# Moving one merge gate's projection from the fourth recurrence head's side work to the third's

## The chip, the cores and the metric

The kernel runs on one core of one Trainium2 chip. The metric is the device time of one execution in microseconds (us), the median of several runs; less is better. A profile of one execution gives what each engine did: PE (matrix multiply), DVE (vector), ACT (scalar and activation), POOL (GpSimd), SP (the engine that issues most transfers).

## What is computed

The kernel is one residual block over 1040 tokens (16 meta tokens and 1024 frames) of width 1024. The reference, cut to what matters here:

```python
u = _rmsnorm(h, norm_g[l])
proj = u @ w_in[l]                       # 6144 columns
(sb_q, sb_k, sb_v, sb_gate, hg_q, hg_f, hg_i, hg_gate, gate_sb, gate_hg) = jnp.split(proj, bounds, -1)
y_sb = _stick_breaking(sb_q, sb_k, sb_v) * jax.nn.silu(sb_gate)
o_hg = _group_rmsnorm(_hgrn2(hg_q, hg_f, hg_i, lb_all[l]), hg_norm_g[l])   # recurrence, 4 heads
y_hg = o_hg * jax.nn.silu(hg_gate)
merged = (jax.nn.sigmoid(gate_sb) * (y_sb @ w_sb_out[l])
          + jax.nn.sigmoid(gate_hg) * (y_hg @ w_hg_out[l]))                # 1024 + 1024 gate columns
h = h + merged @ w_out[l]
```

The recurrence of a head is S_t = diag(f_t) S_{t-1} + (1 - f_t) i_t^T, computed by doubling blocks (1, 4, 16, 32, 64, 128 tokens): each level multiplies keys and queries by products of forget gates on DVE, and forms a few small products on PE.

## The kernel before

Every float32 matrix product is done in three parts (high x high, high x low, low x high), so a weight block of 1024 x 128 columns is fetched raw (`wr`, by SP, L102), copied to its high part (`wh`, ACT L115) and its low part formed (`wl`, POOL L120). `wr`, `wh` and `wl` have two buffers each. A projection's matmuls are L259. A merge gate's projection is 48 matmuls of 512 columns into two PSUM tiles; ACT L994 applies the sigmoid, and L995 stores the result in DRAM. A head's forget-gate projection f is 72 matmuls of about 346 columns; ACT L780/L781 and POOL L783/L782 finish it.

Sixteen merge gates are wanted; ten are left for side work, five of them run beside the attention, and five (columns blocks 3 to 7 of `gate_hg`) beside the four recurrence heads. For each head `recurrence` gives a list of steps (main) and `stream` a list of quanta of three matmuls each (fill); `interleave` weaves the two by weights:

```python
target = base + span * m / total + lead
while fillq and done[0] < target:
    fw, ff = fillq.pop(0)
    ff()
    done[0] += fw
```

The fill of heads 0 to 2 is the next head's f projection and the gates in `some`; the fourth head's is its gates, then `split_all` (high and low parts of the attention's results, ACT L1028 and DVE L1029) and the first two products with `w_sb_out`. `stream` also loads the weights of the group that follows the one that begins. A scheduler then decides each engine's order from this text, and each engine keeps its order strictly.

In a head's main the names are: L858 (PE) the products of the levels 1 and 4 ("quads"), L874 those of level 16, L887 those of levels 32 and 64, L903 and L906 (DVE) the updates of keys and queries after each level, L942 to L950 the states, L962/L963 the outputs, L965 their copy, L834 a clear of the next head's matrix on POOL, L86/L87 a power on POOL, L972 the norm on DVE, L984 the transposes of the outputs in the next head.

After the heads come the products with `w_sb_out` and `w_hg_out`, and last the output product with `w_out` (L1270). The blocks of `w_out` are prepared in `direct(c)`, whose raw rows are fetched into the same two `wr` buffers (L1138), and whose first DVE operation is

```python
V.tensor_tensor(w12, w12, w11, op=ALU.subtract)     # L1150
put(3, BH[:, 3, c], BL[:, 3, c], w12)               # L1143 on ACT, L1144 on DVE
```

`direct` is written after the last head, but the scheduler places its DVE operations inside the third and the fourth head's lists. Its first transfer goes into the `wr` buffer of gate block 6, so it can't start before POOL has read that buffer for the last time (L120).

Of the kernel before, what the change touches and what calls it, by code (L numbers as in the profile page):

```python
# [45 lines left out]
def block_kernel(ctx: ExitStack, tc: tile.TileContext, x, meta, norm_g, w_in, w_sb_out,  # L46
# [218 lines left out]
    def stream(groups, nxt=None):  # L265
        q, pend = [], []
        for i, g in enumerate(groups):
            if "quanta" in g:
                q, pend = q + pend + g["quanta"], []
                continue  # L270
            follow = groups[i + 1] if i + 1 < len(groups) else nxt

            def first(g=g, follow=follow, state=[]):
                if not state:
                    state.append(1)
                    ensure(g)
                    if g["begin"]:
                        g["begin"]()
                    if follow is not None:
                        ensure(follow)  # L280
            qs = []
            for t0, n in g["pieces"]:
                qs += piece_quanta(g, t0, n, first)
            late, pend = pend, g["after"]
            for k, x in enumerate(late):
                qs.insert(4 + 3 * k, x)
            q += qs
        return q + pend
# [8 lines left out]
    def interleave(steps, lead=0.0):  # L297

        for _, fill in steps:
            fillq.extend(fill)  # L300
        for main, fill in steps:
            base = done[1]
            done[1] += sum(w for w, _ in fill)
            total = sum(w for w, _ in main)
            span = done[1] - base
            m = 0.0
            for w, fn in main:
                fn()
                m += w
# [5 lines that stand above are left out]
# [676 lines left out]
    def gate_group(gcol, e):  # L991
        def eg(acc, t0, n):
            sg = sb("sg", [P, 512])
            S.activation(sg, acc, AF.Sigmoid)  # L994
            nc.scalar.dma_start(gates[gcol, e][:, t0 - NM:t0 - NM + n], sg)  # L995

        return proj(gcol + P * e, REAL, eg)
# [88 lines left out]
    rest = [gate_group(C_GS, e) for e in range(N_GS, 8)] + [gate_group(C_GH, e) for e in range(8)]  # L1086
    share = FILL
    side, k0 = [], 0
    for p in range(4):
        own = ([pairs[1][1][1]], pairs[2][1], pairs[3][1], heads[0][1])[p]  # L1090
        some = rest[k0:k0 + share[p]]
        k0 += share[p]
        side.append(own[:1] + some[1:2] + own[1:] + some[:1] + some[2:])
    rest = rest[k0:]
# [12 lines left out]
    def hg_gate(h):  # L1107

        def emit():
            y = yhg[h]  # L1110
            g = sb("q", [P, SEQ])
            nc.sync.dma_start(g, kept_hg[h])
            V.tensor_tensor(y, y, g, op=ALU.mult)
        return (0.0, emit)

    tail = []
    for h in range(4):
        main, t = recurrence(h, heads[h][0], ("q", "ab", "v", "ab")[h])
        main = main[:1] + tail + main[1:]
        tail = t + [hg_gate(h)]  # L1120
        some, rest = (rest[:1], rest[1:]) if h < 3 else (rest, [])
        if h < 3:
            fill = stream(heads[h + 1][1] + some, heads[h + 2][1][0] if h < 2 else (rest + sbg)[0])
        else:
            fill = stream(some, sbg[0]) + [(0.0, split_all)] + stream(sbg[:2], sbg[2])
        interleave([(main, fill)], LEAD_B)
# [216 lines left out]
```

## Time and profile before

| | us |
|---|---|
| median of 3 runs | 902.82 (902.47 to 902.85) |
| the profiled execution | 903.0 |
| its span, first to last instruction | 901.3 |
| PE busy | 875.1 (97%) |
| DVE busy | 626.1 (69%) |

PE busy is an upper bound of real use, since matmuls overlap; but where PE is busy without a hole, what decides a stretch is the number of its matmuls. The profiled execution took 1.7 us more than its span.

### The profile page before, as it was taken

The numbers are of one execution on the slowest core, as the hardware profiler recorded it, in microseconds if no ns is written. First come the engines' busy times: TensorE is split into PE (matmuls) and PEld (weight loads), VectorE is DVE, ScalarE is ACT, GpSimd is POOL, SyncE is SP. The second block draws the span as 40 slices with busy tenths as digits, with TensorE's granted clock in tenths as the row PEclk, the third lists the DMA queues.
The fourth block names the chain that finished last, engine by engine and source line by source line (L and its number), as shares of the span: only waits on it lengthen the run. The fifth ranks groups of instructions, "written<-read, shape, count | busy, mean of one in ns | idle before, by whom it ended". The sixth has DMA issues, their size and how long they took to land. (4 is left out here: it accounts for less than half of the span.)

```text
span 901.3 us, 14988 instructions
## 1 busy us (share of the span) xinstructions
PE 875.1 (97%) x5672; PEld 753.5 (84%) x5672; DVE 626.1 (69%) x1081; ACT 408.0 (45%) x933; POOL 279.4 (31%) x303
## 2 busy tenths in 40 slices
PE   7999999999999999999999999999989999999996
PEld 5998888888889998898998898878877788888885
DVE  6893446555332468789788778867555788897886
ACT  7763333333332456546556556333435363223331
POOL 1026445544442212233211140526342000004552
PEclk9999999999999999999999999999999999999998
DMA  9223543333434312311321311232311466564212
GB/s 283 66 70 97 174 143 109 105 117 106 137 121 137 121 47 72 94 49 46 101 83 55 115 48 36 83 95 83 108 60 48 136 220 218 179 213 146 94 47 95
DMA packets 90587, 98.12 MB, mean 109 GB/s; under 512 B 6017, under 2 KB 65281, under 8 KB 90514
## 3 DMA queue, kind: packets, MB, share of 16 engines
q1 hardware_dynamic: 76688, 73.52, 26.9%
q10 hardware_dynamic: 13826, 23.64, 7.0%
q8 instruction: 45, 0.74, 0.4%
q14 instruction: 28, 0.23, 0.1%
HBM read 71.94 MB, written 25.20 MB: 108 GB/s over the span
## 5 line engine op out<-in xcount | busy, mean ns | idle before, releaser
L259 PE MATMUL acc<-uh,wh 128*128 128x346 f32 (+2 forms) x472 | 174.1, 369 | 0.0
L259 PE MATMUL acc<-ul,wh 128*128 128x346 f32 (+2 forms) x472 | 164.7, 349 | 0.0
L259 PE MATMUL acc<-uh,wl 128*128 128x346 f32 (+2 forms) x472 | 164.5, 349 | 0.0
L120 POOL TENSOR_TENSOR wl<-wr,wh 128x256 fp32r<-128x256 f32 x92 | 76.5, 852 | 281.0 <-ACT wh L115 253.4
L259 PEld LDWEIGHTS acc<-uh,wl 128*128 128x128 f32 x472 | 89.2, 189 | 7.0
L259 PEld LDWEIGHTS acc<-uh,wh 128*128 128x128 f32 x472 | 89.2, 189 | 5.3 <-issue 1.2
L259 PEld LDWEIGHTS acc<-ul,wh 128*128 128x128 f32 x472 | 89.6, 190 | 3.0 <-issue 0.4
L455 POOL TENSOR_TENSOR pw<-su,pw 128x512 fp32r<-128x512 f32 x44 | 59.2, 1367 | 43.3 <-ACT pw L454 43.3
L455 POOL TENSOR_TENSOR pw<-wr,pw 128x512 fp32r<-128x512 f32 x33 | 43.7, 1323 | 61.9 <-ACT pw L454 61.9
L628 ACT ACTIVATE ab<-z 128x456 f32<-128x456 f32 (+6 forms) x112 | 49.8, 448 | 26.5 <-PE z L626 26.0
L631 DVE TENSOR_TENSOR_SCAN ab<-ab,later 128x456 f32<-128x456 f32 (+3 forms) x64 | 55.6, 871 | 6.9 <-ACT ab L628 6.3
L466 PE MATMUL acc<-th,pw 128*128 128x512 f32 x176 | 58.0, 390 | 0.0
L671 DVE TENSOR_TENSOR wt<-tr,wt 128x384 fp32r<-128x384 f32 (+1 forms) x80 | 50.4, 630 | 10.1 <-ACT wt L670 7.9
L670 ACT ACTIVATE wt<-tr 128x384 fp32r<-128x384 f32 (+1 forms) x80 | 44.3, 555 | 26.0 <-PE tr L668 25.8
L682 PE MATMUL av<-wt,v 128*128 128x256 f32 x320 | 52.6, 286 | 3.6 <-DVE sg L689 3.1
L626 PE MATMUL z<-stk,q 128*128 128x456 f32 (+6 forms) x224 | 55.9, 331 | 0.0
L454 ACT ACTIVATE pw<-su 128x512 fp32r<-128x512 f32 x44 | 25.9, 626 | 60.9 <-DVE su L449 35.5
L682 PEld LDWEIGHTS av<-wt,v 128*128 128x128 f32 x320 | 46.2, 188 | 8.2 <-DVE sg L689 5.2
L635 DVE TENSOR_TENSOR_SCAN ab<-ab 128x348 f32<-128x348 f32 (+4 forms) x48 | 47.0, 980 | 7.2 <-ACT ab L628 5.8
L668 PE MATMUL tr<-ident,ab 128*128 128x128 f32 x288 | 45.3, 273 | 0.7 <-DVE ab L631 0.7
L115 ACT ACTIVATE wh<-wr 128x256 fp32r<-128x256 f32 x92 | 34.4, 412 | 22.0 <-PE acc L259 9.9
L626 PEld LDWEIGHTS z<-stk,q 128*128 128x128 f32 x224 | 38.3, 189 | 3.4
(360 smaller groups left out, 2031.1 us busy)
## 6 DMA issues: line engine op xcount, KB each, us to landing
wr<-in_w_in SPq DMA_DIRECT2D x48, 512.0 KB, 4.1
q<-q SPq DMA_DIRECT2D x32, 256.0 KB, 4.3
wr<-in_w_out SPq DMA_DIRECT2D x16, 512.0 KB, 3.6
sg<-gate SPq DMA_DIRECT2D x24, 256.0 KB, 3.4
gate<-sg ACTq DMA_DIRECT2D x20, 256.0 KB, 2.0
xb<-in_x SPq DMA_DIRECT2D x7, 512.0 KB, 8.3
gate<-co ACTq DMA_DIRECT2D x12, 256.0 KB, 2.0
pt<-hi SPq DMA_DIRECT2D x4, 520.0 KB, 3.3
```

Source lines behind the costliest of these rows:

```text
L120: eng.tensor_tensor(lo[:, cs], raw[:, cs], h[:, cs].bitcast(F32), op=ALU.subtract)
L259: T.matmul(acc, a, b, start=(k == 0), stop=(k == total - 1))
L455: G.tensor_tensor(t[:, 1], d[key], t[:, 0].bitcast(F32), op=ALU.subtract)
L466: T.matmul(acc, t[:, part // 2, c], (bh, bl, bh)[part][:, c], start=(c == part == 0), stop=(c == 3 and part == 2))
L626: T.matmul(z, qt[:, k, qo + qi * P:qo + (qi + 1) * P], st["k"][hh][:, c0:c1], start=(k == 0), stop=(k == 1))
L628: S.activation(a[:, c0:c1], z, AF.Sigmoid, scale=-1.0)
L631: ins = V.tensor_tensor_scan(w, w, later[:, WS - (n - c0):][:, ::-1], 1.0, op0=ALU.mult, op1=ALU.max)
L635: V.tensor_tensor_scan(w, w, w, a[:, c1:c1 + 1], op0=ALU.mult, op1=ALU.bypass)
L668: T.transpose(tp[:, c:c + P], self.w[qi][:, s0:s0 + P], ident)
L670: S.activation(wt[:, 0, lo:], tp[:, lo:], AF.Copy)
L671: V.tensor_tensor(wt[:, 1, lo:], tp[:, lo:], wt[:, 0, lo:].bitcast(F32), op=ALU.subtract)
L682: T.matmul(self.av, st["v"][hh][:, 2 * gg + j], wt[:, part, where[j]:where[j] + 256], start=(gg == g and part == 0 and j == 0), stop=False)
```

## The change

One more gate goes with the third head (h = 2), one fewer with the fourth (h = 3); the order of the gates stays.

```diff
         main, t = recurrence(h, heads[h][0], ("q", "ab", "v", "ab")[h])
         main = main[:1] + tail + main[1:]
         tail = t + [hg_gate(h)]
-        some, rest = (rest[:1], rest[1:]) if h < 3 else (rest, [])
+        n = (1,1,2,1)[h]
+        some, rest = rest[:n], rest[n:]
         if h < 3:
             fill = stream(heads[h + 1][1] + some, heads[h + 2][1][0] if h < 2 else (rest + sbg)[0])
```

No operation is added or removed. `interleave` now puts about 10 us more of fill weight (block 6) beside the third head, and the scheduler orders every engine anew from the third head's middle on. Lines after the diff have a number one higher than before: L1150 becomes L1151, L1144 becomes L1145.

On PE in the third head (products of level 16 and 32, `z`; `acc` with `wh_6779` is gate block 5, with `wh_6938` block 6). Before, the level 32 product came three matmuls into block 5's second half:

```order
L259 MATMUL acc_6948<-uh_72,wl_6780 128x512
L799 MATMUL tr_7072<-ident_63,pt_6773 16x128
L259 MATMUL acc_7075<-uh_72,wh_6779 128x512
L259 MATMUL acc_7075<-ul_73,wh_6779 128x512
L259 MATMUL acc_7075<-uh_72,wl_6780 128x512
L887 MATMUL z_7079<-wt_6313,stk_6310 32x32 x16
L259 MATMUL acc_7075<-uh_72,wh_6779 128x512
```

Now the level 16 product comes 21 matmuls into that half (the last four are shown):

```order
L259 MATMUL acc_7034<-uh_72,wl_6780 128x512
L259 MATMUL acc_7034<-uh_72,wh_6779 128x512
L259 MATMUL acc_7034<-ul_73,wh_6779 128x512
L259 MATMUL acc_7034<-uh_72,wl_6780 128x512
L874 MATMUL z_7056<-wt_6313,stk_6310 32x16 x32
L259 MATMUL acc_7034<-uh_72,wh_6779 128x512
L259 MATMUL acc_7034<-ul_73,wh_6779 128x512
L259 MATMUL acc_7034<-uh_72,wl_6780 128x512
L259 MATMUL acc_7115<-uh_72,wh_6938 128x512
```

Block 5's and block 6's other matmuls follow, so 18 matmuls stand between L874 and the level 32 product, and the small products come later against the fill.

On DVE in the third head (`stk` keys, `wt` queries, `wr_7820` the first raw rows of `w_out`). Before, the subtraction of `direct` stood ahead of the update of level 16:

```order
L903 TENSOR_TENSOR stk_6310<-stk_6310,ab_6761 128x65x8
L906 TENSOR_TENSOR wt_6313<-wt_6313,ab_6761 128x64x8
L866 COPY_PREDICATED dg_6758<-mask_651_4110,z_6952 128x16x12
L866 COPY_PREDICATED dg_6758<-mask_651_4110,z_6952 128x16x8
L866 COPY_PREDICATED dg_6758<-mask_651_4110,z_6952 128x16x4
L1150 TENSOR_TENSOR wr_7820<-wr_7820 128x512
L903 TENSOR_TENSOR stk_6310<-stk_6310,ab_6761 128x32x16
L906 TENSOR_TENSOR wt_6313<-wt_6313,ab_6761 128x32x16
```

Now it stands ahead of the updates of level 4:

```order
L908 TENSOR_TENSOR ab_6761<-ab_6761 128x8
L1151 TENSOR_TENSOR wr_7820<-wr_7820 128x512
L903 TENSOR_TENSOR stk_6310<-stk_6310,ab_6761 128x130x4
L906 TENSOR_TENSOR wt_6313<-wt_6313,ab_6761 128x128x4
L903 TENSOR_TENSOR stk_6310<-stk_6310,ab_6761 128x65x8
L906 TENSOR_TENSOR wt_6313<-wt_6313,ab_6761 128x64x8
```

It moved up by four updates and three masked copies. POOL's list is the same in both, row for row.

On DVE in the fourth head (`wr_7833` the next raw rows of `w_out`, L926 and L947 of the states), the second subtraction now stands like this; before, it stood ahead of L926, and L947 had other work before it:

```order
L1145 TENSOR_TENSOR ul_7819<-wr_7822,uh_7818 128x512
L903 TENSOR_TENSOR stk_6772<-stk_6772,ab_7291 128x8x64
L906 TENSOR_TENSOR wt_6775<-wt_6775,ab_7291 128x8x64
L1145 TENSOR_TENSOR ul_7819<-wr_7820,uh_7818 128x512
L926 COPY v_7635<-tr_7636 16x128
L1054 TENSOR_TENSOR pt_7488<-acc_7512,sg_7302 128x256
L1151 TENSOR_TENSOR wr_7833<-wr_7833 128x512
L947 COPY stk_7652<-av_7653 128x128
```

Its buffer is the one that the first row shown here reads last.

## Rows read from the trace of the kernel before

**Rows 1.** The page, busy time: engine, us, share of the span, instructions.

```profile
PE 875.1 (97%) x5672; PEld 753.5 (84%) x5672; DVE 626.1 (69%) x1081; ACT 408.0 (45%) x933; POOL 279.4 (31%) x303
```

**Rows 2.** Windows, third and fourth head: length, engines' busy us, granted clock, DMA share, GB/s.

```profile
645.60:692.00 46.40, 42.11 (x453) 35.08 (x452) 27.55 (x53) 19.12 (x49) 17.82 (x17) 0.96 0.20 66
692.00:748.60 56.60, 55.59 (x499) 44.87 (x499) 46.26 (x94) 25.19 (x66) 5.03 (x5) 1.00 0.51 168
```

**Rows 3.** Waits of PE, 640 to 760 us: total us, times, longest.

```profile
PE z L887 <- DVE wt L906: 3.7, 1, 3.7
PE tr L984 <- DVE ab L972: 1.6, 2, 1.0
```

**Rows 4.** Chain of waits (whole, and of 660 to 680 us): start, us, what.

```profile
665.04 2.09 POOL wl L120 x3
...
667.15 4.27 DMA wr<-in_w_out
...
673.46 0.70 PE z L887 x32
...
748.61 66.84 PE acc L259 x288
```

**Rows 5.** Windows around two waits of PE; columns as in rows 2.

```profile
669.75:673.46 3.71, 0.00 (x1) 0.01 (x1) 1.95 (x4) 0.00 (x0) 0.00 (x0) 1.00 0.06 25
674.08:677.53 3.45, 3.45 (x15) 2.67 (x9) 1.29 (x2) 2.02 (x6) 0.00 (x0) 0.53 0.20 78
696.20:699.20 3.00, 1.99 (x73) 1.61 (x72) 3.00 (x4) 1.10 (x2) 0.00 (x0) 1.00 0.23 87
```

**Rows 6.** Timeline of PE in the third head.

```profile
652.14 0.66 PE L984 MATMUL tr<-ident,ab 128*128 128x128 f32 x4 [0.58 <-DVE ab L972]
...
660.44 0.40 PE L259 MATMUL acc<-uh,wh 128*128 128x512 f32 x1
...
668.80 0.48 PE L259 MATMUL acc<-uh,wh 128*128 128x512 f32 x1
...
674.08 0.66 PE L259 MATMUL acc<-uh,wh 128*128 128x512 f32 x1
...
677.93 1.15 PE L887 MATMUL z<-wt,stk 128*64 128x64 f32 x16
```

**Rows 7.** Timeline of POOL in the third head.

```profile
653.64 0.62 POOL L782 TENSOR_SCALAR stk<-stk,omlb,lb 128x348 f32<-128x348 f32 x1
...
661.03 0.74 POOL L120 TENSOR_TENSOR wl<-wr,wh 128x256 fp32r<-128x256 f32 x1 [1.31 <-ACT wh L115]
...
662.88 2.16 POOL L782 TENSOR_SCALAR stk<-stk,omlb,lb 128x346 f32<-128x346 f32 x1
```

**Rows 8.** Timeline of DVE in the third head.

```profile
654.15 1.23 DVE L1113 TENSOR_TENSOR ab<-ab,q 128x1024 f32<-128x1024 f32 x1 [0.51 <-ACT ab L985]
...
659.42 1.00 DVE L908 TENSOR_TENSOR ab<-ab 128x65 f32<-128x65 f32 x4
...
664.01 0.68 DVE L906 TENSOR_TENSOR wt<-wt,ab 128x512 f32<-128x512 f32 x1
...
671.51 0.69 DVE L1150 TENSOR_TENSOR wr<-wr 128x512 f32<-128x512 f32 x1 [5.92 <-DMA wr<-in_w_out]
```

**Rows 9.** Timelines of the fourth head: PE, DVE, SP's queue, ACT.

```profile
697.41 1.09 PE L984 MATMUL tr<-ident,ab 128*128 128x128 f32 x8 [1.01 <-DVE ab L972]
...
708.52 0.89 PE L858 MATMUL z<-wt,stk 128*32 128x48 f32 x64
...
704.57 0.45 DVE L848 TENSOR_TENSOR wt<-wt,ab 128x256 f32<-128x256 f32 x1
...
707.12 0.76 DVE L120 TENSOR_TENSOR wh<-wl,wh 128x256 fp32r<-128x256 f32 x2
...
721.28 2.14 SPq L1138 DMA_DIRECT2D wr<-in_w_out  x2
...
725.48 0.63 ACT L1143 ACTIVATE uh<-wr 128x512 fp32r<-128x512 f32 x1 [0.65 <-DMA wr<-in_w_out]
```

## The prediction, made before the changed kernel ran

> **What bounds the kernel now.** I began with the page: PE is busy 97% of the span [rows 1], so most of the time is set by the number of its matmuls, which the change leaves alone. What it can move is holes in PE, and the rate at which matmuls go. So I read the stretch of the heads next, by windows. The third head's window has 46.40 us with PE busy 42.11, and it alone shows a granted clock below 1.00 [rows 2]. The fourth has PE busy 55.59 of 56.60, with DVE busy 46.26, so there DVE has 10.3 us to spare. The waits of PE in this stretch name three holes, all ended by DVE: one of 3.7 us ahead of L887 and two ahead of L984, 1.6 us together, the larger 1.0 [rows 3]. After the last head PE runs 288 matmuls back to back in 66.84 us [rows 4], 0.232 us each; this step of a 512-column matmul is used below.
>
> The chain of waits tells where the 3.7 us come from [rows 4]: POOL ends three L120 (low parts of gate block 6's weights) at 667.13; only then is their raw buffer free, and SP's transfer of `w_out` rows takes 4.27 us into it; DVE, whose next instruction in order is L1150, stands still for it for 5.92 us and starts it at 671.51 [rows 8]; behind it come the two updates, and the level 32 product starts at 673.46 [rows 4]. PE had run out of matmuls placed ahead of that product.
>
> The hole costs more than itself. In the window of the hole PE does nothing for 3.71 us; in the next, 674.08 to 677.53, the granted clock is 0.53, so mostly the lower level, 1.2 GHz, in place of 2.4 [rows 5]. Nine matmuls fill 674.08 to 677.93 [rows 6]: 3.85 us, where nine steps of 0.232 and some 0.2 for the changes between block kinds make 2.3. That is 1.5 us lost. Around the fourth head's hole of 1.0 us the clock stays at 1.00 [rows 5].
>
> **The change, part by part.** It adds no instruction and removes none, no transfer either: 48 matmuls (11.1 us of PE) stand in the third head rather than the fourth. PE's total is the same, so the sum is made of holes and of the slow clock.
>
> *The third head's first hole* (0.58 us ahead of L984 [rows 6]). L984 now comes after 15 matmuls of the second piece of f rather than 8; the seven more, of 346 columns, are over 1 us of work. DVE is ready at the old time, since nothing ahead of it moved. Gain 0.6 us.
>
> *The third head's large hole.* DVE's subtraction moved up by four updates, so DVE waits longer; what counts is when it is released and what PE still has then. f's last matmul is followed by the first of block 5 at 660.44 [rows 6]; without the first hole that is 659.9. From there to the first L120 of block 6 POOL needs 0.6 us, and to the start of L782 another 1.85 [rows 7]: 662.3. L782 took 2.16 us here and 0.62 for 348 columns at 653.64. The longer one ended at 665.04, as L906 of DVE (from 664.01, 0.68) ended its run of four updates [rows 8]; at 653.64 to 654.15 DVE was idle but for 0.1 us [rows 8]. In the new order DVE stands waiting from about 661 (its small products ended at 660.42 [rows 8], and L1113 ahead of them moves back by some 0.5), so no update runs beside L782: I take 0.62. Then three L120, 2.1 us, to 665.0, and the transfer, 4.27, to 669.3. From the release of L1150 to the small product took 671.51 to 673.46, 1.95 us, with two updates between [rows 4, 8]; now four stand between, at 0.61 each two more: 3.2 us. L874 can start at 672.6. PE gets there when? Block 5's first half with its small blocks took 660.44 to 668.80, 8.36 us [rows 6], of which one small block of the kind of L887's 0.70 [rows 4] now stands later: 7.6. Then 21 matmuls, 4.9: 659.9 + 12.5 = 672.4. So a hole of 0.2 us in place of 3.7, with no slow clock, since even 1.0 us brought none. If L782 takes 2.16 all the same, the hole is 1.7. Gain 3.7 + 1.5 - 0.2 = 5.0 us; low end 3.5 less a slow clock if it comes, 2.0; high end 5.2.
>
> The Trainium skill, page SBUF — State Buffer, section SBUF: two separate sides, says that POOL and a DVE operation with two SBUF inputs take one pair of ports by an exclusive lock, the loser blocked for the whole instruction. The two rows of L782 agree with it; without such a rule the sum would keep 2.16 and stand 1.5 us higher.
>
> *The fourth head's hole ahead of L984* (1.01 [rows 9]). It lies between L832 and L984, with the chain POOL clear, POOL power, L972 between, and 15 matmuls to cover it, in both orders. No change.
>
> *The fourth head's thinner cover.* Here the 48 matmuls are missing, and DVE's chain meets PE at more places. Ahead of the second product of quads there were 39 matmuls after L984, 11.1 us to L858 [rows 9]; 12 fewer make 8.3. DVE ended L848 at 705.02, 7.6 us after L984 began; now two L120 (0.68 in steps [rows 9]) stand ahead too: 8.3. A hole of 0 to 0.2, I take 0.1. Between L874 and the second L887 PE has 21 matmuls, 4.9 us, and the first L887; DVE has some 14 operations, five of them updates or low parts more than the chain needs, about 6.0 against 5.7: 0.3. Last, the second subtraction: SP's transfer was issued at 721.28 and first used at 725.48, 4.2 us later [rows 9]; DVE now reaches it 2.4 us after the buffer is free, so it waits about 1.8 us ahead of L947 and the states. PE has its transposes and some 10 matmuls there, about as much as DVE needs: 0.3, and up to 1.8 if these come out shorter. Together 0.7 us, from 0 to 2.5.
>
> *After the heads* the same matmuls follow in the same order. DVE is a few low parts behind there, some 2 to 3 us; three PSUM tiles of 2.8 us each stand between it and PE. I cost it at nothing; if that cover is gone, it costs up to 1 us.
>
> The sum: 903.0 - 0.6 - 5.0 + 0.7 = 898.1. The profiled execution stood 0.2 us above the median, so the median should be **898.0** (rounded up), 0.53% below 902.8. A difference of 0.2% (1.8 us) is about what a measurement of this kernel can tell from no change.
>
> **Rivals.**
> 1. *POOL stays slow*, or the transfer lands 1.5 us later than 4.27: a hole of 1.7 us ahead of L874. 899.5 without the slow clock, 901.0 with it. For it: L782 ran 2.16 once; against it: DVE has nothing to run beside it in the new order. Chance 0.14.
> 2. *The fourth head's waits add up*: three close places with errors the same way, and the second subtraction at its upper price: 899.7, or 901.2 if one of them lets the clock fall. For it: DVE at 46.26 of 56.60 [rows 2], in a window that loses 11.1 us. Chance 0.13.
> 3. *Slower: DVE becomes the bound of the fourth head.* If all of its 10.3 us of idle time stayed (waits for PE's small products, POOL's power, the transfer), the head would not get shorter at all by the matmuls that left: 903 - 5.6 + 11.1 = 908.5. The point from which it decides: the head would take 46.3 us and what stays of the idle, against 45.5 in the sum; over 6.6 us of the 10.3 must stay to end above 904.6. Against it: six or so of the low parts of `w_out` and two of the attention's results leave that stretch of DVE's list. Chance 0.04.
> 4. *No change*: the wait only goes to another place, DVE standing at L1151 until some 676 rather than 669.3, a hole ahead of L874 of 3.7 us with its slow clock, 903 less the 0.6: 902 to 903. It needs a release 3.5 us later than my steps give, such as another transfer ahead of this one in SP's queue; before, the queue waited for nothing but the buffer. Chance 0.05.
>
> **Numbers.** The forecast, the hole gone and 0 to 1.5 us given back in the fourth head (897.0 to 899.3), has 0.64. Range 896.8 to 901.0: it takes in the first two rivals but for their worst ends, and leaves out about 0.15. Faster by over 0.2% (below 901.0): 0.64, nearly all of the first rival and most of the second: 0.84. Within 0.2%: 0.12. Slower: 0.04.
>
> **What would show it.** In the profile after: the third head's window at clock 1.00 with no hole over 0.5 us; DVE idle ahead of L1151 for some 8 us, longer than before; L782 beside it at 0.6 to 0.9; the transfer issued near 665 and landed near 669; L874 near 672.5; the fourth head with PE's hole of 1.0 ahead of L984, and small ones ahead of L858, L887 and L963. Wrong would be: a clock below 1.00 in either head, a hole of over 1.5 us ahead of L874, or DVE's second wait for `w_out` followed by a hole of PE.

## The result and the profile after

The changed kernel takes **897.4 us** (median of 4 runs, 896.82 to 899.36) against 902.84 of the kernel before (4 runs beside it, 902.47 to 904.4): ratio 0.9939, 95% interval 0.9925 to 0.9953. The forecast was 898.0, its range 896.8 to 901.0. The profiled execution took 896.8, with a span of 895.1, 6.2 us less than the 901.3 of before.

The page's busy times (us, share of the span, instructions) answer to [rows 1], the waits of PE from 640 to 760 us (in all, times, longest) to [rows 3]:

```profile
PE 873.3 (98%) x5672; PEld 752.4 (84%) x5672; DVE 625.9 (70%) x1081; ACT 406.9 (45%) x933; POOL 279.2 (31%) x303
```

```profile
PE tr L984 <- DVE ab L972: 1.1, 1, 1.1
```

The wait of 3.7 us ahead of L887 is gone, and of the two ahead of L984 the fourth head's alone is left. The windows of the two heads, cut at the same instructions as [rows 2] (length, then PE, PEld, DVE, ACT, POOL, clock, DMA share, GB/s):

```profile
645.30:694.80 49.50, 49.50 (x493) 41.50 (x492) 28.32 (x53) 20.17 (x51) 17.50 (x17) 1.00 0.23 78
694.80:742.30 47.50, 46.31 (x459) 37.30 (x459) 41.26 (x88) 22.34 (x64) 5.47 (x5) 1.00 0.48 156
```

Before, the heads took 46.40 + 56.60 = 103.0 us; now 49.5 + 47.5 = 97.0. Nearly the whole difference arises here: the third head begins 0.3 us earlier (645.30 against 645.60), which the change does not explain, and behind the fourth head 152.7 us were left before (901.3 - 748.6), and 152.8 are now (895.1 - 742.3). Of the 48 matmuls, 40 cross the cut between the two windows (x453 to x493, x499 to x459), which is 9.3 us of PE. The third head has PE busy in all of its 49.50 us, at clock 1.00 where it had been 0.96.

The steps of the prediction can be followed in the timelines of PE, POOL, SP's queue and DVE, in this order:

```profile
652.23 0.60 PE L984 MATMUL tr<-ident,ab 128*128 128x128 f32 x4
...
671.81 0.74 PE L874 MATMUL z<-wt,stk 128*32 128x16 f32 x64
...
700.25 0.66 PE L984 MATMUL tr<-ident,ab 128*128 128x128 f32 x4 [1.09 <-DVE ab L972]
...
656.76 2.19 POOL L782 TENSOR_SCALAR stk<-stk,omlb,lb 128x346 f32<-128x346 f32 x1
...
661.83 0.63 POOL L782 TENSOR_SCALAR stk<-stk,omlb,lb 128x346 f32<-128x346 f32 x1
662.43 2.11 POOL L120 TENSOR_TENSOR wl<-wr,wh 128x256 fp32r<-128x256 f32 x3
...
664.57 0.33 SPq L1139 DMA_DIRECT2D wr<-in_w_out  x1
...
657.93 0.68 DVE L906 TENSOR_TENSOR wt<-wt,ab 128x512 f32<-128x512 f32 x1
...
668.06 0.69 DVE L1151 TENSOR_TENSOR wr<-wr 128x512 f32<-128x512 f32 x1 [7.33 <-issue]
...
670.49 0.68 DVE L906 TENSOR_TENSOR wt<-wt,ab 128x512 f32<-128x512 f32 x1
...
724.53 0.42 DVE L1054 TENSOR_TENSOR pt<-acc,sg 128x256 f32<-128x256 f32 x1 [1.03 <-PE av L940]
724.87 0.68 DVE L1151 TENSOR_TENSOR wr<-wr 128x512 f32<-128x512 f32 x1
```

DVE's wait for `w_out` did not go away: it is longer than before, 7.33 us against 5.92 [rows 8], and PE does not wait behind it. The trace puts it down to "issue"; I take the transfer issued at 664.57 and first read at 668.06 for what ended it, since the subtraction reads nothing but its rows.

### The profile page after: what moved, and what is told of

Same layout as the page of the kernel before. It is cut to its first block, busy times and chain, and to the rows that moved or that the text cites. A ratio compares the mean times of both kernels' runs of the same rounds, so it can differ in the third digit from the quotient of the medians.

```text
span 895.1 us, 14985 instructions
## 1 busy us (share of the span) xinstructions
PE 873.3 (98%) x5672; PEld 752.4 (84%) x5672; DVE 625.9 (70%) x1081; ACT 406.9 (45%) x933; POOL 279.2 (31%) x303
## 4 chain that ended last, share of the span: by engine, by line
PE 86%; DVE 8%; ACT 3%; issue 1%; POOL 1%; DMA 1%; ACTq 0%; DVEq 0%; POOLq 0%
PE acc L259 34%; PE acc L466 10%; PE z L466 7%; PE tr L466 7%; PE acc L1271 4%; PE av L682 3%; PE tr L668 3%; PE z L626 3%; PE tr L1271 3%; PE z L1271 2%; PE acc L350 2%; DVE ab L635 2%; DVE ab L631 1%; PE z L963 1%; PE z L962 1%
## 5 line engine op out<-in xcount | busy, mean ns | idle before, releaser
L259 PE MATMUL acc<-uh,wh 128*128 128x346 f32 (+2 forms) x472 | 173.4, 367 | 0.0
L259 PE MATMUL acc<-ul,wh 128*128 128x346 f32 (+2 forms) x472 | 164.1, 348 | 0.0
L259 PE MATMUL acc<-uh,wl 128*128 128x346 f32 (+2 forms) x472 | 163.6, 347 | 0.0
L120 POOL TENSOR_TENSOR wl<-wr,wh 128x256 fp32r<-128x256 f32 x92 | 76.0, 846 | 273.4 <-ACT wh L115 245.7
L259 PEld LDWEIGHTS acc<-uh,wl 128*128 128x128 f32 x472 | 88.8, 188 | 6.8
L259 PEld LDWEIGHTS acc<-uh,wh 128*128 128x128 f32 x472 | 88.9, 188 | 4.7 <-issue 0.8
L259 PEld LDWEIGHTS acc<-ul,wh 128*128 128x128 f32 x472 | 89.2, 189 | 3.3 <-issue 0.8
```

Source lines behind the costliest of these rows:

```text
L120: eng.tensor_tensor(lo[:, cs], raw[:, cs], h[:, cs].bitcast(F32), op=ALU.subtract)
L259: T.matmul(acc, a, b, start=(k == 0), stop=(k == total - 1))
```

## Experiments

The theory: the gain is the hole of 3.7 us that DVE's wait for `w_out` left in PE, with the slow clock behind it and the small hole ahead of the third head's L984; the longer third head covers the wait. The rivals: more matmuls in the third head are worth something for themselves; the wait only changes its place. All ratios stand against runs of the kernel before on the same chip (902.84 us for the changed kernel, 903.32 for the first four runs, 903.47 for the last three), so runs of different rows are compared by their ratios.

| | us (runs) | ratio, 95% interval |
|---|---|---|
| changed kernel | 897.40 (4) | 0.9939, 0.9925 to 0.9953 |
| one: before, subtraction held | 898.28 (5) | 0.9945, 0.9933 to 0.9958 |
| two: changed, subtraction held | 897.63 (5) | 0.9942, 0.9929 to 0.9954 |
| three: gates 1, 1, 3, 0 | 910.47 (5) | 1.0078, 1.0064 to 1.0091 |
| four: gates 1, 0, 2, 2 | 901.09 (11) | 0.9976, 0.9967 to 0.9984 |
| five: gates 1, 2, 1, 1 | 900.75 (5) | 0.9968, 0.9956 to 0.9981 |
| six: three updates more | 899.96 (6) | 0.9965, 0.9953 to 0.9977 |
| seven: six updates more | 903.64 (11) | 0.9996, 0.9986 to 1.0006 |

**One: take the wait away and leave the gates.** In the kernel before, the first `direct` is held back until the fourth head's first DVE operation has been issued (lines from there on carry numbers one or two higher):

```diff
+            if hd == 3:
+                late.append(ins)
...
-        direct(e - 4)
+        if e == 4:
+            with tc.issue_after(late[0].ins):
+                direct(0)
+        else:
+            direct(e - 4)
```

> The gates stay as before (one, one, one, two); only the first subtraction of w_out and what follows it are held back until the fourth head's first DVE operation, so the third head's DVE list holds no wait for a transfer. Theory (the gain is the hole of 3.7 us at that wait and the slow clock behind it, 1.5): the hole ahead of L887 and the clock of 0.53 are gone, the 0.6 us ahead of the third head's L984 stays, so 902.8 - 5.2 = 897.6, up to 899 where the fourth head pays for the subtraction. Rival (the gain comes from 48 more matmuls in the third head, whatever DVE waits for there): 902 to 903.

898.28 us, and the ratio cannot be told from the changed kernel's. The waits of PE (640 to 760 us), the windows of the third and the fourth head, and the timelines of PE and DVE:

```profile
PE tr L986 <- DVE ab L974: 1.6, 2, 1.0
```

```profile
645.70:687.00 41.30, 40.71 (x458) 34.06 (x457) 27.19 (x52) 19.11 (x49) 17.85 (x17) 1.00 0.22 74
687.00:743.80 56.80, 55.67 (x499) 44.74 (x499) 46.74 (x95) 25.20 (x66) 5.07 (x5) 1.00 0.52 168
```

```profile
652.32 0.66 PE L986 MATMUL tr<-ident,ab 128*128 128x128 f32 x4 [0.59 <-DVE ab L974]
...
701.62 0.68 DVE L1152 TENSOR_TENSOR wr<-wr 128x512 f32<-128x512 f32 x1
```

The hole ahead of the level 32 product is gone without moving a gate, the 0.59 ahead of the third head's transposes stays, and the subtraction, now in the fourth head, waits for nothing. The third head takes 41.30 us against 46.40, at a clock of 1.00, and the fourth is as long as before. The transfer itself is issued at 667.34, as before (667.15), so what moved is DVE's place for it. So the gain is the wait's, not that of the third head's added matmuls.

**Two: the same hold in the changed kernel** (gates 1, 1, 2, 1).

> The changed kernel with the same hold: DVE no longer stands 7.3 us at the subtraction in the third head. Theory (the longer third head covers that wait, it costs nothing): the time of the changed kernel, 897.4, within 0.2%. Rival (the covered wait still takes something, later in DVE's list or in the clock): 895.5 or less. On the side: if the 0.63 us of L782 comes from DVE standing idle beside it, it takes about 2.1 us here, beside DVE's updates, and if it comes from something else, 0.63 again.

897.63 us: the covered wait costs nothing that these runs can tell. The question on the side came out against the reason that I gave. DVE and POOL in the third head:

```profile
665.35 0.70 DVE L905 TENSOR_TENSOR stk<-stk,ab 128x520 f32<-128x520 f32 x1 [4.25 <-PE z L860]
...
662.21 0.63 POOL L782 TENSOR_SCALAR stk<-stk,omlb,lb 128x346 f32<-128x346 f32 x1
```

L782 takes 0.63 us here too, but DVE does not update beside it: without the subtraction it waits 4.25 us for the second product of quads (L860 with the hold, L858 in the kernels without it), which the added matmuls have moved behind L782.

**Three: all three gates in the third head, none in the fourth** (`n = (1,1,3,0)[h]`).

> All three remaining gates' matmuls in the third head, none in the fourth. The fourth head's stretch of 45.3 us loses another 11.1 us of PE, to 34.2, with DVE busy for 39.1 there in the changed kernel, of which some 3 are low parts that leave with the gate. Theory (a head costs the longer of PE and DVE's busy time plus a few small waits): the stretch takes 37 to 40, the kernel 900.5 to 903.5. Rival 3 of the prediction (DVE's idle time there stays whole): the stretch stays at 45.3, the kernel at 908. If the matmuls leave without a price: 897.4.

910.47 us: my theory missed by 7 us, and rival 3's 908 is near. The heads' windows, with the same columns as above, then the waits of PE (700 to 760 us), and the chain behind the largest on ACT, POOL and PE:

```profile
645.70:706.80 61.10, 61.10 (x542) 50.60 (x541) 31.48 (x59) 23.72 (x59) 17.98 (x17) 1.00 0.27 87
706.80:754.20 47.40, 39.79 (x420) 30.89 (x420) 38.22 (x84) 17.89 (x53) 5.30 (x5) 0.96 0.38 116
```

```profile
PE tr L984 <- DVE ab L972: 4.6, 2, 3.2
PE acc L259 <- DVE wt L1029: 1.5, 1, 1.5
```

```profile
710.85 0.31 ACT L969 ACTIVATE sg<-ab 128x128 f32<-128x128 f32 x1 [2.74 <-DMA gate<-sg]
...
712.65 0.20 POOL L86 TENSOR_SCALAR s<-s 128x8 f32<-128x8 f32 x1 [4.12 <-ACT sg L969]
...
715.92 0.77 PE L984 MATMUL tr<-ident,ab 128*128 128x128 f32 x5 [3.24 <-DVE ab L972]
```

The third head grew by the gate, 49.5 to 61.1; the fourth did not get shorter, 47.4 against 47.5. But DVE is not full there (38.22 of 47.40); PE stands idle for 7.6 us (1.2 in the changed kernel), and the clock falls to 0.96. The largest hole ends a chain: the last gate's store out of `sg` is issued only at 706.15, just before the head begins; ACT waits 2.74 us for it before it may write its sums of squares into `sg`, POOL's power comes behind these, then L972, then PE. In the changed kernel the chain has no such wait, beside about as many matmuls (15 there, 14 here), and costs 1.09 us against 3.24. The matmuls that stand here in place of a gate's are products with `w_sb_out`, which wait for DVE themselves (the 1.5 ahead of L259), and five more waits, of 0.31 to 1.34 us, join. That a gate's matmuls would have covered all of these is argued; no run takes them one by one.

**Four: none in the second head, two in the third and fourth** (`n = (1,0,2,2)[h]`).

> The third head keeps two gates as in the changed kernel, the fourth has two as before, the second none. The first subtraction of w_out stands later in DVE's list. Theory: no hole at a wait for w_out; the second head (38.6 us, PE 37.9, DVE 24.9) goes to 27.5 of PE, less than the busy time of DVE and the small waits of its chain allow: 897.4 plus 1 to 4 us of holes there, 898.4 to 901.4. Rival (the spread of the gates alone decides, two in the third are enough): 897.4.

901.09 us, within the theory's 898.4 to 901.4: two gates in the third head are not enough by themselves. PE waits 1.13, 0.25 and 0.92 us in the second head and 1.72 ahead of the third's L984; no wait of PE for `w_out` is among them. The theory had put all of the holes into the second head; what lengthened the 1.72 was not tried.

**Five: the fourth head's gate to the second** (`n = (1,2,1,1)[h]`).

> The fourth head's gate goes to the second head, the third keeps one as before. The first subtraction of w_out then stands at the third head's start in DVE's list, ahead of the first products of gates. Theory (the gain is the wait that leaves the place ahead of L887, wherever the gate goes): no hole ahead of L887 and a clock of 1.00; the second head's hole ahead of L984 (0.7) goes as well, the third's of 0.6 stays: 897 to 898.5. Rival (a wait for w_out only changes its place): a hole ahead of the third head's L984 of 2 us or more, 900 to 903.

900.75 us, which is the rival's outcome, though not by its cause. POOL at the third head's start, and DVE and PE behind it:

```profile
657.26 0.95 POOL L834 MEMSET ab<- 128x1024 f32 x1
658.18 1.92 POOL L120 TENSOR_TENSOR wl<-wr,wh 128x256 fp32r<-128x256 f32 x2
660.18 0.20 POOL L86 TENSOR_SCALAR s<-s 128x8 f32<-128x8 f32 x1
...
662.19 1.23 DVE L972 TENSOR_TENSOR ab<-ab,s 128x1024 f32<-128x1024 f32 x1 [3.38 <-POOL s L87]
663.55 0.74 DVE L1151 TENSOR_TENSOR wr<-wr 128x512 f32<-128x512 f32 x1
...
663.47 1.12 PE L984 MATMUL tr<-ident,ab 128*128 128x128 f32 x4 [2.31 <-DVE ab L972]
```

The subtraction waits for nothing. But the added gate's low parts, two L120 of 1.92 us together, now stand in POOL's list between the clear and the power, so L972 is late and PE has a hole of 2.31 us, with a slow clock behind it. ACT's last sum was there at 658.64 and the power started at 660.18, so these low parts account for some 1.5 us of the hole. Where a gate goes decides what its side work collides with; the wait for `w_out` was removed here as well.

**Six and seven: a hole of chosen length.** In the changed kernel, three or six more updates ahead of the third head's L874 (each x = max(x, x) on the queries, which changes no value):

```diff
+            if hd == 2 and h == 4:
+                for _ in range(3):
+                    V.tensor_tensor(qv, qv, qv, op=ALU.max)
```

> The changed kernel with three more updates of 0.61 us each (x = max(x, x) on the queries, values unchanged) on DVE ahead of the third head's L874. With the three masked copies that now stand ahead too (0.67), DVE releases L874 2.5 us later; some 0.6 us were to spare, so a hole of 1.9 us. Theory (the clock falls behind long holes only: 1.72 us left it at 1.00 in the run with no gate in the second head, 3.24 and 3.71 did not): clock 1.00, 897.5 + 1.9 = 899.4. Rival (any hole longer than those of 1.0 to 1.1 us costs the clock too): 900.9.

> The same with six: L874 4.5 us later, a hole of 3.9 us. Theory (a hole as long as the one of before takes the clock with it, another 1.5 us): the granted clock near 0.53 for about 3.5 us behind the hole, 897.5 + 3.9 + 1.5 = 902.9. Rival (a hole costs only itself, and the 1.5 us had another cause): 901.4.

PE's L874 in the timeline, and the window behind the hole, with three more updates:

```profile
674.20 0.74 PE L874 MATMUL z<-wt,stk 128*32 128x16 f32 x64 [1.75 <-DVE wt L906]
```

```profile
674.00:678.00 4.00, 3.80 (x78) 3.21 (x79) 1.85 (x5) 2.14 (x6) 1.49 (x2) 1.00 0.15 56
```

The same with six, in two windows:

```profile
677.95 1.06 PE L874 MATMUL z<-wt,stk 128*32 128x16 f32 x64 [4.04 <-DVE wt L906]
```

```profile
678.00:680.00 2.00, 2.00 (x67) 1.77 (x68) 0.93 (x2) 0.00 (x0) 0.48 (x1) 0.50 0.26 37
680.00:684.00 4.00, 4.00 (x12) 2.88 (x10) 0.57 (x2) 1.66 (x4) 0.00 (x0) 0.62 0.31 117
```

The kernel before took 0.6 us more on this chip than beside the changed kernel, so the changed kernel's 897.4 stands for some 898.0 here. Against that, a hole of 1.75 us left the clock at 1.00 and cost some 2 us (its runs spread over 898.6 to 901.3, so nothing beyond the hole is settled). One of 4.04 us cost 5.6: the 1.6 beyond itself is not measured closely, but the slow clock, 2 x 0.50 + 4 x 0.38 = 2.5 us by the windows, is enough for it. Run six bears out its theory by the clock, its time lying between the two outcomes; run seven does so by both. A hole like the one of before, put back in another place, gives back the whole gain: 903.64 against 903.47.

## Why the prediction was right

*The third head's first hole*, 0.6: gone, as said, at 652.23. In run one, with fewer matmuls ahead of it, it stays at 0.59; the times of the two kernels cannot tell so little apart.

*The third head's large hole*, 5.0: right in mechanism and nearly in size. Against the steps: L782 0.63 us (0.62 taken), the transfer issued at 664.57 (665.0), L1151 at 668.06 (669.3), L874 at 671.81 with no hole (672.6, after a hole of 0.2). The step that is off is the transfer: first read 3.5 us after its issue, not 4.27. The 4.27 was on the slow side: in the trace of the kernel before, the sixteen transfers of L1138 land 3.4 to 5.1 us after their issue, with a median of 3.6. (By its own terms the step gives L874 at 669.3 + 3.2 = 672.5, not 672.6, and a hole of 0.1.) DVE ended L906 at 671.2, 0.6 us ahead of L874, so PE's list and not DVE set its start. Rival 1 fell with L782, and rival 4 with the release. Runs one and seven show the term from both sides: without the hole and its clock the old order is worth 898.28, and with a like hole the new one 903.64.

*Why L782 was short.* Here the step's reason was only half right. I had DVE stand at the subtraction; run two shows it standing there for L858's product without any subtraction. The row that the step rests on holds: in the same trace the L782 at 656.76 lies beside four updates of DVE and takes 2.19, the one at 661.83 lies beside an idle DVE and takes 0.63, and runs one (2.16) and two (0.63) fit. The long ones end when DVE's run does: the fourth update ends at 664.69 in the kernel before and L782 at 665.04 [rows 7, 8], not with it as I had read; now they end at 658.61 and 658.95. The distance is 0.35 and 0.34 us. The Trainium skill, page SBUF — State Buffer, section SBUF: two separate sides, has an exclusive lock between POOL and a DVE operation with two SBUF inputs, and these rows agree that POOL is held up beside such operations. That one L782 is held over several of them and not over one is what these rows alone show.

*The fourth head's thinner cover*, 0.7: the step that was mis-sized. Nothing of it came; PE waits there only the 1.09 ahead of L984 (1.01 taken). At L858 PE arrived just as DVE was done: L848 ends at 708.57, L858 starts at 708.71. Ahead of the second L887 DVE had its update done at 719.81, and PE came to it at 720.23, so the 0.3 of that place is nothing too. For the second subtraction I expected a wait of 1.8 us for its transfer. SP issued that at 721.10, and DVE came to it at 724.87, 3.8 us later, after it had waited 1.03 us for PE's product `av` (the row of L1054 above); by then the rows had landed, so a wait for PE, which I had not counted, hid the end of a transfer that was also quicker than my 4.2. The sum without this term and the 0.2 at L874 is 903.0 - 0.6 - 5.2 = 897.2, against 896.8 of the profiled execution; 0.3 of the rest lies ahead of the third head. With one gate less still, run three, the fourth head does not shrink at all, as rival 3 had it for this change: the cover that I called thin was enough here, and none of it is too little. Rival 3's price was set with 11.1 us leaving the fourth head; 9.3 did.

*How near the number is* is in part luck. By the profiled executions the gain is 6.2 us, and the sum had 4.9. The median moved by 5.4, because the profiled execution of before lay 0.2 above its median and the one of now lies 0.6 below.

*After the heads*, nothing: 152.7 and 152.8 us.

## What to carry to other kernels

A wait costs what the engine at the bound cannot cover, and not its length: here it grew from 5.92 to 7.33 us and its price fell from 5.2 to nothing that the runs can tell, because PE still had matmuls when it ended. So before moving work, look for the one instruction that waits in a list in which others are urgent; holding it back (run one) gave the same gain as moving a gate, without thinning another stage. And side work is cover: in runs three to five, which moved it further or elsewhere, holes opened at chains over several engines, which the stage's busy times do not show.

## What the runs showed of the hardware

The clock did not fall behind every hole of PE. Behind holes of 1.0 to 1.1 us, of 1.72 (run four) and of 1.75 (run six) it stayed at 1.00; behind holes of 2.31 (run five), 3.24 (run three, with a hole of 1.48 us shortly before it), 3.71 [rows 5] and 4.04 us (run seven) it fell to 0.50, half of full speed, so 1.2 GHz in place of 2.4. Behind the 1.72 of run four, then behind the 3.24 of run three:

```profile
650.20:653.00 2.80, 2.76 (x20) 2.76 (x21) 2.80 (x5) 1.27 (x2) 2.51 (x2) 1.00 0.00 0
...
715.90:717.90 2.00, 1.98 (x52) 1.71 (x56) 2.00 (x6) 1.27 (x2) 0.00 (x0) 0.72 0.10 28
717.90:719.90 2.00, 2.00 (x38) 1.63 (x28) 1.79 (x5) 0.00 (x0) 0.00 (x0) 0.50 0.28 103
```

The length of the slow stretch differed: for run five some 3 us, for run seven 5, as the windows show that begin in run five where L984 starts, and above for run seven:

```profile
663.47:665.50 2.03, 2.03 (x9) 1.97 (x10) 1.91 (x3) 0.69 (x1) 1.94 (x2) 0.50 0.00 0
665.50:667.50 2.00, 2.00 (x55) 1.76 (x57) 0.92 (x3) 0.69 (x1) 0.00 (x0) 0.69 0.00 0
667.50:670.00 2.50, 2.50 (x49) 2.44 (x36) 2.50 (x4) 0.01 (x1) 0.00 (x0) 1.00 0.22 62
```

Its price was 1.6 us in run five (2.03 x 0.50 + 2.00 x 0.31), 1.5 in the kernel before and 2.5 in run seven. On how the clock decides, the runs say no more than that.
